# Four modulation vectors moved to VectorE column sums, a third direct tile in each SwiGLU, and ScalarE making half of the modulated inputs

## The chip, the cores and the metric

One core of one Trainium2 chip runs the whole program in one launch. The metric is the device time of one execution in microseconds; before the change it is 2919.62 us, the median of 3 runs (2915.01 to 2922.16). Engines are called TensorE (PE in the rows, its weight loads PEld), VectorE (DVE), ScalarE (ACT), GpSimd (POOL) and the DMA queue of SyncE (SP).

## What is computed

Two post-norm layers over 512 latent and 256 context tokens of 1024 channels. Each layer is a half-step SwiGLU, a token mixer (a bidirectional gated DeltaNet beside a Conformer convolution in layer 0, "even"; grouped-query attention in layer 1, "odd"), and a second SwiGLU; all in float32 precision.

```python
def ffn_sublayer(x, shift, scale, gate, w_gu, w_down, g, b):
    y = swiglu(modulate(x, shift, scale), w_gu, w_down)      # x * (1 + scale) + shift
    return layer_norm(ALPHA * x + 0.5 * gate * y, g, b)
def adaln_modulation(cond, w_ada, b_ada):                    # nine vectors of 1024 per layer
    return jnp.split(silu(cond) @ w_ada + b_ada, 9, axis=-1)
```

There are two conditioning vectors, one for latent and one for context tokens, so that each of the 18 modulation vectors (9 per layer) is a 2x1024 product with a 1024x1024 block of `ada_w` (4 MB).

## The kernel before, in words

The program is first recorded as a list of operations and then ordered by a list scheduler (`Program.order`, L265): it walks all five engines with a price for each operation (`price`, L188), takes the ready one of the lowest rank, and writes one fixed order per engine. Where its plan leaves TensorE idle for too long it puts in a filler, a 128x128 float32 matmul of the identity into a spare piece of PSUM (`keep`; `pair<-ident` in the rows), which computes nothing that is used. All instructions are emitted at L516, so one reads the rows by tile names and shapes: `b` is a PSUM bank, `pair` a spare PSUM tile (fillers also write to it), `p` a page of SBUF, `mods` the modulation vectors, `cA` and `cB` the scale and shift that the modulation uses.

A product in float32 precision is made of three float32r matmuls (`mm3`): high by high, high by low, low by high. So every operand is first split by `halves` (L703) into a high part (ScalarE copies it) and a low part (VectorE subtracts).

**A SwiGLU** (`ffn`, L1095) has 22 inner tiles of 128 channels. The first HEAD = 2 are made directly (`up`): 8 x 2 x 3 matmuls of 256 columns for each of three chunks of 256 tokens (context C_, latents L1 and L2; the last SwiGLU has no context and two chunks). They can start as soon as one chunk of the input is modulated. The other 20 are made by a Strassen-like scheme (`unit`, L1056): 7 block products x 4 x 3 = 84 matmuls of 384 columns (256 in the last SwiGLU). It needs `Blocks` (L612): sums and differences of the whole modulated input, each split into halves, on VectorE and ScalarE; and per unit `left`, which does the same to the weights. Before `Blocks`, the input pages are stored to DRAM (`xd`), and each finished inner tile is stored too (`hd`). Then comes the down projection: three groups of up to six inner tiles, 8 output tiles each, 18 matmuls of 384 columns per output and half, added to the input by VectorE (`residual`). In the tail, the last four inner tiles are multiplied chunk by chunk, and each chunk is normalized (`normalize`) and modulated (`modulate`, L1008) for what follows.

**The modulation vectors** are made in three ways. `ada` (L793) makes the first two. `ada_sum` (L820) scales the eight 128x1024 pieces of `ada_w` on VectorE by the conditioning column and accumulates them (8 operations of 128x1024 per condition), and then sums over the 128 partitions on TensorE: 4 matmuls with 32 columns of ones and 512 moving columns, a ScalarE copy, 4 transposes, 2 to 4 small VectorE adds. It is a generator whose steps are handed out one per unit and one per output tile of the down projection (`extra`), at rank 100 behind their place. `ada_mm` (L854) does the whole product on TensorE: 16 matmuls of 32x512 with the condition as weights, a copy, 4 transposes, an add; it is used inside the two mixers, where VectorE and ScalarE have the smaller matmuls between them.

**`modulate`** writes for each k of 8 channel tiles a plain copy m = z*a+b (GpSimd for three of four k, VectorE for every fourth), the high part of the same (ScalarE), then per pair of k the low part (VectorE, m minus high), and last scales z itself on GpSimd.

Of the kernel before, what the change touches and what calls it, by code (L numbers as in the profile page):

```python
# [13 lines left out]
AF = mybir.ActivationFunctionType  # L14
ALU = mybir.AluOpType
# [98 lines left out]
def cols(v):  # L114
    return math.prod(v.shape[1:])


class Program:
# [69 lines left out]
    def price(self, o):  # L188

        a, f = o.a, o.f  # L190
        o.bytes = 0
        if f == "matmul":
            n = cols(a[2])
            if a[0].shape[0] == 32 and a[1].shape[0] == 128 and "skip_group_check" in o.k:
                return 0.02 + n * 0.00047
            if a[1].dtype == F32R:
                return max(0.112, 0.0045 + n * 0.000442)
            return 0.01 + max(n, cols(a[1])) * 0.00168
        if f == "transpose":
            return max(0.03, a[1].shape[0] * 0.00086)  # L200
        if f == "dma_start":
            o.bytes = math.prod(a[0].shape) * 4
            return 0.45
        n = cols(a[0])
        if f == "tensor_reduce":
            n = cols(a[1])
        psum = any(isinstance(v, View) and v.tile.pool == "psum" for v in a)
        if o.eng == "vector":
            two = sum(isinstance(v, View) for v in a) > 2
            if f in ("tensor_scalar", "memset", "tensor_copy") and not psum and not two:  # L210
                return 0.14 + n * 0.0006
            return 0.15 + n * 0.00104 + 0.05 * (f == "scalar_tensor_tensor")
        if o.eng == "scalar":
            c = 0.168 + n * 0.00084 if psum else 0.205 + n * 0.000825
            return c + 0.17 * isinstance(o.k.get("scale"), View) + 0.37 * ("accum_out" in o.k)
        if f == "memset":
            return 0.03 + n * 0.0009
        return 0.37 + n * 0.0007 if f == "tensor_scalar" else 0.155 + n * 0.0022
# [313 lines left out]
L1 = (CTX, 256, 0)  # L532
# [9 lines left out]
R_ADA, R_WEIGHT, M_POOL = 100, 150, 4  # L542
T_POOL, S_POOL = False, False

HEAD, GROUP, TAIL, EARLY_U = 2, 6, 4, 2


class Feat:
# [116 lines left out]
class Net:  # L665
# [154 lines left out]
    def ada_sum(self, l, i, conds=2):  # L820

        nc = self.nc
        w = self.io["ada_w"][l].rearrange("(k p) n -> k p n", p=128)
        acc = []
        for k in range(8):
            raw = self.page()
            nc.sync.dma_start(raw, w[k, :, 1024 * i:1024 * i + 1024])
            for m in range(conds):
                c = self.cond[:, k, m:m + 1]
                if k == 0:  # L830
                    acc.append(self.page())
                    nc.vector.tensor_scalar(acc[m], raw, c, None, op0=ALU.mult)
                else:
                    nc.vector.scalar_tensor_tensor(acc[m], raw, c, acc[m], op0=ALU.mult, op1=ALU.add)
            yield
        ps = self.bank()
        for e in range(2):
            for m in range(conds):
                q = conds * e + m
                nc.tensor.matmul(ps[32 * q:32 * q + 32, :], self.ones32, acc[m][:, 512 * e:512 * e + 512], start=True, stop=True, skip_group_check=True)  # L840
        P = 64 * conds
        sb = self.page()
        nc.scalar.activation(sb[0:P, 0:512], ps[0:P, :], AF.Copy)
        pt = self.bank()
        for j in range(4):
            nc.tensor.transpose(pt[:, 128 * j:128 * j + P], sb[0:P, 128 * j:128 * j + 128], self.ident[0:P, 0:P])
        for e in range(2):
            for m in range(conds):
                q = conds * e + m
                o = 8 * i + 4 * e  # L850
                nc.vector.tensor_tensor(self.mods[l][:, m, o:o + 4], pt.rearrange("p (j x) -> p x j", x=128)[:, 32 * q, :], self.adab[:, l, o:o + 4], op=ALU.add)
        yield

    def ada_mm(self, l, i):  # L854
# [153 lines left out]
    def modulate(self, c0, n, cond, A, B, ag, ab, tiles=(0, 8)):  # L1008

        nc = self.nc  # L1010
        for p in range(tiles[0] // 2, tiles[1] // 2):
            z = self.xa.pair(p, c0, n)
            h, l = self.xh.pair(p, c0, n), self.xl.pair(p, c0, n)
            m = self.xm.pair(p, c0, n) if self.xm else self.wide(2 * n).rearrange("p (s n) -> p s n", s=2)
            for s in range(2):
                k = 2 * p + s
                a, b = A[:, cond, k:k + 1], B[:, cond, k:k + 1]
                (nc.gpsimd if k % M_POOL else nc.vector).tensor_scalar(m[:, s], z[:, s], a, b, op0=ALU.mult, op1=ALU.add)
                nc.scalar.activation(h[:, s], like(z[:, s], h[:, s]), AF.Identity, scale=a, bias=b)
            nc.vector.tensor_tensor(l, like(m, h), h.bitcast(F32), op=ALU.subtract)  # L1020
            if ag is None:
                nc.gpsimd.tensor_scalar(z, z, ALPHA, 0.0, op0=ALU.mult, op1=ALU.add)
            else:
                for s in range(2):
                    k = 2 * p + s
                    nc.gpsimd.tensor_scalar(z[:, s], z[:, s], ag[:, k:k + 1], ab[:, k:k + 1], op0=ALU.mult, op1=ALU.add)
# [1079 lines left out]
class Kernel(Even, Odd, Final, Net):  # L2106
# [13 lines left out]
    def run(self):  # L2120
        split = [C_, L1, L2]
        self.nc.epoch("p6", 10)
        self.setup()
        A, B = self.small([128, 2, 8], "cA"), self.chunk(0, 0)
        self.new_x()
        for q in range(4):
            k = slice(2 * q, 2 * q + 2)
            self.ada(q, None if q else self.params)
            self.nc.vector.tensor_scalar(A[:, :, k], self.chunk(0, 1)[:, :, k], 1.0, None, op0=ALU.add)
            for c0, n, cond in split:  # L2130
                if not q:
                    self.load_x(range(6)[c0 // 128:(c0 + n) // 128])
                self.modulate(c0, n, cond, A, B, None, None, (k.start, k.stop))
        self.ffn(0, 0, split, 2, self.sub(0, 0, (0, 3)), self.ada_sums(0, 2, 3, 4))
        self.nc.epoch("p4", 16)
        self.even_params()
        self.even(split, self.sub(0, 1, (0, 6)), chain(*(self.ada_mm(0, i) for i in (5, 6, 7, 8))))
        self.nc.epoch("p6", 10)
        self.ffn(0, 1, split, 8, self.sub(0, 2, (1, 0)), self.ada_sums(1, 0, 1, 2))
        self.ffn(1, 0, split, 2, self.sub(1, 0, (1, 3)), self.ada_sums(1, 3, 4, 5))  # L2140
        self.nc.epoch("p4", 16)
        self.odd([L1, L2], self.sub(1, 1, (1, 6)), chain(*(self.ada_mm(1, i) for i in (6, 7, 8))))
        self.ffn(1, 1, None, 8, None, iter(()))
        self.nc.keep = self.nc.tensor.matmul(self.keep, self.ident, self.ident, start=True, stop=True)

# [30 lines left out]
```

## Time and profile before

| | |
|---|---|
| median of 3 runs | 2919.62 us |
| the profiled execution | 2922.82 us |
| its span, first to last instruction | 2921.1 us |
| TensorE busy | 2855.0 us, 98% |
| TensorE weight loads busy | 2654.4 us, 91% |
| VectorE, ScalarE, GpSimd busy | 2050.3, 1124.0, 541.6 us |
| DMA engines, mean busy share | 38%, 119 GB/s |

In the rows below, a group of instructions gives its count behind the x, then the busy time of the group, the mean duration of one, and the idle time before them. A float32 matmul is two records (two passes), a float32r matmul and a transpose are one. Matmuls overlap in the array, so busy time over count is what one costs, not the mean duration. Fillers count as busy TensorE time.

### The profile page before, as it was taken

The page shows a single profiled execution, that of the slowest core. Times are in us where ns is not written, and L with a number is a line of the kernel's source. Part 1 is how long each engine was busy: PE and PEld are TensorE (multiplying, and loading weights), DVE is VectorE, ACT ScalarE, POOL GpSimd, SP SyncE. Part 2 cuts the span into 40 slices and gives each one's busy share as a digit, 9 for nine tenths or more (in the row PEclk, how much of TensorE's full clock was granted, in tenths as well). Part 3 has the DMA queues.
Part 4 walks back from the last instruction along what each step waited for, and adds up shares of the span by engine and source line. Part 5 has one row for each costly group of instructions (what it writes and reads, how often), then busy time and mean ns, then how long its engine had stood idle before and what let it go on. Part 6 is the DMA issues. An engine that isn't in the chain of part 4 may idle for free.

```text
span 2921.1 us, 48213 instructions
## 1 busy us (share of the span) xinstructions
PE 2855.0 (98%) x19173; PEld 2654.4 (91%) x19173; DVE 2050.3 (70%) x3549; ACT 1124.0 (38%) x1952; POOL 541.6 (19%) x652
## 2 busy tenths in 40 slices
PE   9999999999999999999999999999999999999999
PEld 7999999988777899999999999999998777899998
DVE  4877674578877777877675587786547666788854
ACT  4443332143334634443332244343114454455522
POOL 3000000244863605000000230000007331310001
PEclk9999999999999999999999999999999999999999
DMA  7544373134633223344362144345412331144541
GB/s 236 159 135 124 124 214 100 32 116 116 177 94 105 92 80 123 100 129 139 114 220 88 30 146 128 116 136 195 135 49 63 94 129 49 50 139 134 163 130 48
DMA packets 386014, 346.94 MB, mean 119 GB/s; under 512 B 38528, under 2 KB 338813, under 8 KB 385789
## 3 DMA queue, kind: packets, MB, share of 16 engines
q1 hardware_dynamic: 385789, 343.86, 38.0%
q8 instruction: 151, 2.47, 0.4%
q14 instruction: 74, 0.61, 0.1%
HBM read 296.33 MB, written 47.48 MB: 118 GB/s over the span
## 4 chain that ended last, share of the span: by engine, by line
PE 74%; DVE 5%; DMA 2%; POOL 2%; ACT 1%; issue 1%; SPq 0%; DVEq 0%; POOLq 0%; ACTq 0%
PE b L516 70%; PE pair L516 4%; DVE p L516 3%; POOL p L516 2%; ACT p L516 1%; DMA hd<-p 1%; DVE nwt L516 1%; SPq L516 0%; DVE lnS L516 0%; DVE pair L516 0%; DMA xd<-p 0%; DMA p<-hd 0%; DMA p<-in_ffn_w_gu_dram 0%; DMA p<-in_attn_w_out_dram 0%; DMA p<-inv 0%
## 5 line engine op out<-in xcount | busy, mean ns | idle before, releaser
L516 PE MATMUL b<-p,p 128*128 128x384 f32 (+3 forms) x15509 | 2447.5, 317 | 25.9 <-DVE p L516 18.2
L516 PEld LDWEIGHTS b<-p,p 128*128 128x128 f32 x15509 | 2328.1, 189 | 137.1 <-issue 44.6
L516 ACT ACTIVATE p<-p 128x1024 fp32r<-128x1024 f32 (+10 forms) x887 | 708.2, 821 | 1116.1 <-DVE p L516 463.6
L516 DVE TENSOR_TENSOR p<-p,p 128x1024 fp32r<-128x1024 f32 (+6 forms) x942 | 883.1, 959 | 302.2 <-PE b L516 150.5
L516 ACT ACTIVATE p<-b 128x384 f32<-128x384 f32 (+8 forms) x566 | 257.4, 469 | 554.7 <-PE b L516 514.4
L516 POOL TENSOR_TENSOR p<-p 128x512 f32<-128x512 f32 (+1 forms) x26 | 29.9, 1156 | 1535.3 <-ACT p L516 1534.2
L516 DVE SCALAR_TENSOR_TENSOR p<-b,gate,p 128x256 f32<-128x256 f32 (+1 forms) x417 | 168.1, 434 | 201.9 <-PE b L516 201.3
L516 DVE TENSOR_TENSOR p<-p,b 128x384 f32<-128x384 f32 (+3 forms) x392 | 221.8, 581 | 72.8 <-PE b L516 63.5
L516 POOL TENSOR_TENSOR p<-p,p 128x512 f32<-128x512 f32 (+18 forms) x167 | 150.6, 905 | 441.0 <-DMA p<-row 318.4
L516 DVE SCALAR_TENSOR_TENSOR p<-p,cond,p 128x1024 f32<-128x1024 f32 x119 | 150.6, 1279 | 22.4 <-DMA p<-in_ada_w_dram 22.3
L516 PE MATMUL pair<-ident 128*128 128x128 f32 x952 | 131.9, 284 | 9.9 <-DVE pair L516 3.6
L516 PEld LDWEIGHTS pair<-ident 128*128 128x128 f32 x952 | 119.8, 196 | 18.8 <-DVE pair L516 4.9
L516 DVE SCALAR_TENSOR_TENSOR pair<-p,dw,pair 128x783 f32<-128x783 f32 x116 | 120.0, 1035 | 6.9 <-PE pair L516 4.5
L516 POOL TENSOR_SCALAR p<-p,lnag 128x256 f32<-128x256 f32 x112 | 106.8, 962 | 0.3 <-POOL p L516 0.2
L516 DVE TENSOR_TENSOR p<-b,p 128x128 f32<-128x128 f32 (+4 forms) x160 | 68.1, 459 | 52.3 <-ACT p L516 33.2
L516 PEld LDWEIGHTS b<-ident,p 128*128 128x128 f32 (+3 forms) x550 | 63.6, 147 | 37.7 <-issue 16.6
L516 PE MATMUL b<-ident,p 128*128 128x128 f32 (+3 forms) x550 | 87.1, 277 | 10.0 <-DVE p L516 6.4
L516 PE MATMUL pair<-p,p 128*128 128x256 f32 (+3 forms) x515 | 92.2, 315 | 0.0
L516 DVE TENSOR_TENSOR p<-p 128x512 f32<-128x512 f32 (+1 forms) x94 | 63.2, 675 | 34.6 <-PE b L516 32.7
L516 PEld LDWEIGHTS pair<-p,p 128*128 128x128 f32 x515 | 77.2, 190 | 4.6 <-DVE p L516 0.8
L516 PE MATMUL b<-p,ones 128*32 128x128 f32 (+2 forms) x840 | 73.1, 312 | 2.4 <-DVE p L516 1.5
L516 PE MATMUL b<-p,cond 128*32 128x512 f32 (+1 forms) x352 | 69.8, 549 | 5.3 <-DMA p<-in_ada_w_dram 4.9
(168 smaller groups left out, 1135.6 us busy)
## 6 DMA issues: line engine op xcount, KB each, us to landing
p<-in_ffn_w_gu_dram SPq DMA_DIRECT2D x176, 512.0 KB
p<-in_ada_w_dram SPq DMA_DIRECT2D x144, 512.0 KB
p<-in_ffn_w_down_dram SPq DMA_DIRECT2D x96, 384.0 KB
hd<-p SPq DMA_DIRECT2D x54, 384.0 KB
p<-hd SPq DMA_DIRECT2D x27, 768.0 KB
p<-in_even_w_in_dram SPq DMA_DIRECT2D x25, 512.0 KB
xd<-p SPq DMA_DIRECT2D x24, 512.0 KB
p<-xd SPq DMA_DIRECT2D x24, 512.0 KB
```

The lines of the kernel that those rows point to most:

```text
L516: i = f(*[real(x) for x in o.a], **{k: real(x) for k, x in o.k.items()})
```

## The change

- HEAD goes from 2 to 3: in each SwiGLU one inner tile is made directly instead of by a unit.
- `ada_sum` ends in columns: per condition 8 matmuls with a 128x128 block of the sums as weights and one column of ones as the moving operand. They write the vector where the add wants it, so the copy, the transposes and all but one of the adds are gone.
- Four vectors go from `ada_mm` to `ada_sum`: 5 and 6 of layer 0 (from the even mixer to the first SwiGLU), 6 and 7 of layer 1 (from the attention to the SwiGLU ahead of it). 3, 4 and 5 of layer 1 move one SwiGLU: the second SwiGLU makes 0 to 4 of layer 1, the third 5 to 7.
- `modulate` makes m for k = 0, 1, 4, 5 on ScalarE, the others on GpSimd; none on VectorE.
- Two prices of the scheduler change: the 32x512 matmuls, and matmuls of one moving column.

```diff
-                return 0.02 + n * 0.00047
+                return 0.02 + n * (0.00047 if n <= 256 else 0.00085)
...
-            return 0.01 + max(n, cols(a[1])) * 0.00168
+            return 0.01 + (max(n, cols(a[1])) if n > 1 else 64) * 0.00168
...
-HEAD, GROUP, TAIL, EARLY_U = 2, 6, 4, 2
+HEAD, GROUP, TAIL, EARLY_U = 3, 6, 4, 2
...
         ps = self.bank()
-        for e in range(2):
-            for m in range(conds):
-                q = conds * e + m
-                nc.tensor.matmul(ps[32 * q:32 * q + 32, :], self.ones32, acc[m][:, 512 * e:512 * e + 512], ...)
-        ...
+        for m in range(conds):
+            for j in range(8):
+                o = 8 * m + j
+                nc.tensor.matmul(ps[:, o:o + 1], acc[m][:, 128 * j:128 * j + 128], self.ones32[:, 0:1], ...)
+        o = slice(8 * i, 8 * i + 8)
+        nc.vector.tensor_tensor(self.mods[l][:, 0:conds, o], ps[:, 0:8 * conds]..., self.adab[:, l, None, o]..., op=ALU.add)
...
-                (nc.gpsimd if k % M_POOL else nc.vector).tensor_scalar(m[:, s], z[:, s], a, b, op0=ALU.mult, op1=ALU.add)
+                if k % 4 < 2:
+                    nc.scalar.activation(m[:, s], z[:, s], AF.Identity, scale=a, bias=b)
+                else:
+                    nc.gpsimd.tensor_scalar(m[:, s], z[:, s], a, b, op0=ALU.mult, op1=ALU.add)
...
-        self.ffn(0, 0, split, 2, self.sub(0, 0, (0, 3)), self.ada_sums(0, 2, 3, 4))
+        self.ffn(0, 0, split, 2, self.sub(0, 0, (0, 3)), self.ada_sums(0, 2, 3, 4, 5, 6))
-        self.even(split, self.sub(0, 1, (0, 6)), chain(*(self.ada_mm(0, i) for i in (5, 6, 7, 8))))
+        self.even(split, self.sub(0, 1, (0, 6)), chain(*(self.ada_mm(0, i) for i in (7, 8))))
-        self.ffn(0, 1, split, 8, self.sub(0, 2, (1, 0)), self.ada_sums(1, 0, 1, 2))
-        self.ffn(1, 0, split, 2, self.sub(1, 0, (1, 3)), self.ada_sums(1, 3, 4, 5))
+        self.ffn(0, 1, split, 8, self.sub(0, 2, (1, 0)), self.ada_sums(1, 0, 1, 2, 3, 4))
+        self.ffn(1, 0, split, 2, self.sub(1, 0, (1, 3)), self.ada_sums(1, 5, 6, 7))
-        self.odd([L1, L2], self.sub(1, 1, (1, 6)), chain(*(self.ada_mm(1, i) for i in (6, 7, 8))))
+        self.odd([L1, L2], self.sub(1, 1, (1, 6)), chain(*(self.ada_mm(1, i) for i in (8,))))
```

The scheduler then writes a new order for every engine. On TensorE, at the start of the block products of the second SwiGLU, the order before has fillers between the first units (numbers are buffer numbers; a bank `b` is one block product):

```order
L516 MATMUL b_11100<-p_1423_10432,p_1558_11119 128x384
L516 MATMUL b_11100<-p_1423_10432,p_1557_11081 128x384
L516 MATMUL b_11100<-p_1427_10499,p_1557_11081 128x384
L516 MATMUL b_11100<-p_1423_10432,p_1558_11119 128x384
L516 MATMUL pair<-ident_70 128x128 x11
L516 MATMUL b_11111<-p_1529_11163,p_1540_11054 128x384
L516 MATMUL b_11111<-p_1528_11093,p_1541_11091 128x384
L516 MATMUL b_11111<-p_1528_11093,p_1540_11054 128x384
```

and of the change, at the same place, the direct products of 256 columns run up to the first block product:

```order
L516 MATMUL b_11248<-p_1414_10556,p_1502_10741 128x256
L516 MATMUL b_11248<-p_1414_10556,p_1504_10863 128x256
L516 MATMUL b_11248<-p_1418_10590,p_1504_10863 128x256
L516 MATMUL b_11248<-p_1414_10556,p_1505_10882 128x256
L516 MATMUL b_11328<-p_1411_10474,p_1541_11102 128x384
L516 MATMUL b_11328<-p_1415_10506,p_1541_11102 128x384
L516 MATMUL b_11328<-p_1411_10474,p_1542_11142 128x384
```

Behind these rows no filler stands until the down projection. In TensorE's whole order there are 476 fillers before and 430 now; among the block products of the four SwiGLUs 74 before and 6 now, elsewhere 402 and 424.

Also on TensorE, the sums of `ada_sum` stand between block products, one by one. Of before, in the first SwiGLU (`ones` are the weights):

```order
L516 MATMUL b_2158<-p_142_1100,ones_6_76 32x512
L516 MATMUL b_2112<-p_21_646,p_288_2018 128x384
L516 MATMUL b_2158<-p_143_1160,ones_6_76 32x512
L516 MATMUL b_2112<-p_21_646,p_287_1977 128x384
L516 MATMUL b_2158<-p_142_1100,ones_6_76 32x512
```

and of the change (the page `p_154` or `p_155` with the sums is now the weights):

```order
L516 MATMUL b_2262<-p_21_659,p_298_2202 128x384
L516 MATMUL b_2283<-ones_6_76,p_154_1245 128x1
L516 MATMUL b_2262<-p_25_678,p_298_2202 128x384
L516 MATMUL b_2283<-ones_6_76,p_154_1245 128x1
L516 MATMUL b_2262<-p_21_659,p_299_2264 128x384
L516 MATMUL b_2283<-ones_6_76,p_155_1260 128x1 x2
```

Each matmul with one moving column brings a weight block of its own. In all, 34 matmuls of 32x512 with ones and 64 with the condition are gone, 184 of one column are new, and 52 transposes are gone (32 of 128 columns, 20 of 64).

On VectorE, near the end of the first SwiGLU's down projection, residual additions (`gate`) follow each other before:

```order
L516 SCALAR_TENSOR_TENSOR p_468_3184<-b_4575,gate_3192,p_468_3184 128x128
L516 SCALAR_TENSOR_TENSOR p_471_3301<-b_4575,gate_3192,p_471_3301 128x256
L516 SCALAR_TENSOR_TENSOR p_468_3184<-b_4600,gate_3192,p_468_3184 128x128
L516 SCALAR_TENSOR_TENSOR p_471_3301<-b_4600,gate_3192,p_471_3301 128x256
L516 SCALAR_TENSOR_TENSOR p_468_3184<-b_4621,gate_3192,p_468_3184 128x128
L516 SCALAR_TENSOR_TENSOR p_471_3301<-b_4621,gate_3192,p_471_3301 128x256
```

and now scaled sums of `ada_sum` (`cond`) stand between them:

```order
L516 SCALAR_TENSOR_TENSOR p_463_3349<-b_4685,gate_3237,p_463_3349 128x256
L516 TENSOR_TENSOR cB_4712<-cB_4712,mods_9_216 128x16
L516 TENSOR_TENSOR cA_4708<-cA_4708,lngb_186 128x16
L516 SCALAR_TENSOR_TENSOR p_602_4579<-p_615_4688,cond_74,p_602_4579 128x1024
L516 SCALAR_TENSOR_TENSOR p_603_4613<-p_615_4688,cond_74,p_603_4613 128x1024
L516 SCALAR_TENSOR_TENSOR p_460_3221<-b_4710,gate_3237,p_460_3221 128x128
L516 SCALAR_TENSOR_TENSOR p_463_3349<-b_4710,gate_3237,p_463_3349 128x256
```

Between the first and the last residual addition of the first and of the second SwiGLU there are 14 such sums before and 44 now, in the third 7 and 8. Over the whole program there are 42 more of them (161 instead of 119), and the `ada_w` loads of the moved vectors (eight of 512 KB each) move with them; their number and size stay.

## Rows read from the trace of the kernel before

**Rows 1.** The page: busy time by engine, and the granted TensorE clock in 40 slices.

```profile
PE 2855.0 (98%) x19173; PEld 2654.4 (91%) x19173; DVE 2050.3 (70%) x3549; ACT 1124.0 (38%) x1952; POOL 541.6 (19%) x652
PEclk9999999999999999999999999999999999999999
```

**Rows 2.** Busy time by stretch: a down projection, the even mixer, the attention.

```profile
core 0: us, PE busy (x) PEld busy (x) DVE busy (x) ACT busy (x) POOL busy (x), PEclk, DMA share, GB/s
400.00:560.00 160.00, 160.00 (x981) 155.48 (x980) 87.10 (x152) 29.84 (x30) 4.14 (x4) 1.00 0.26 81
660.00:960.00 300.00, 292.49 (x1910) 233.09 (x1910) 238.12 (x290) 117.86 (x232) 179.10 (x238) 0.99 0.42 118
2300.00:2560.00 260.00, 246.71 (x1653) 199.60 (x1652) 171.01 (x480) 126.64 (x300) 74.63 (x63) 0.99 0.26 82
```

**Rows 3.** Groups of TensorE by shape, in units (1260:1440) and in the last SwiGLU (2720:2870).

```profile
L516 PE MATMUL b<-p,p 128*128 128x384 f32 x1002 | 176.4, 337 | 0.3 <-ACT p L516 0.3
L516 PE MATMUL b<-p,p 128*128 128x256 f32 x1275 | 150.4, 281 | 0.0
```

**Rows 4.** TensorE around the start of the units: stretches, and the fillers in them.

```profile
1140.00:1180.00 40.00, 37.01 (x256) 0.96 0.58 178
1700.00:1733.00 33.00, 28.56 (x205) 1.00 0.65 216
...
L516 PE MATMUL pair<-ident 128*128 128x128 f32 x60 | 7.7, 283 | 0.0
L516 PE MATMUL pair<-ident 128*128 128x128 f32 x49 | 6.3, 275 | 0.0
```

**Rows 5.** The chain that ended last, 1150:1175: start, duration, what.

```profile
1154.11 5.33 DMA xd<-p
...
1162.92 6.48 DMA hd<-p
1169.40 0.02 issue
1169.42 1.77 DVE p L516
1171.19 0.04 issue
1171.24 3.12 PE b L516 x11
```

**Rows 6.** Groups by shape, whole run: TensorE's fillers, modulation matmuls and transposes.

```profile
L516 PE MATMUL pair<-ident 128*128 128x128 f32 x952 | 131.9, 284 | 9.9 <-DVE pair L516 3.6 <-ACT p L516 2.8 <-DVE p L516 1.7
L516 PE MATMUL b<-ident,p 128*128 128x128 f32 x498 | 80.3, 281 | 10.0 <-DVE p L516 6.4 <-POOL p L516 1.1 <-DVE inv L516 0.7
L516 PE MATMUL b<-p,cond 128*32 128x512 f32 x224 | 54.8, 605 | 1.0 <-DMA p<-in_ada_w_dram 1.0
L516 PE MATMUL b<-p,ones 128*32 128x512 f32 x68 | 32.4, 605 | 0.0
L516 PE MATMUL b<-ident,p 64*128 64x64 f32 x40 | 5.0, 237 | 0.0
```

**Rows 7.** Timeline of weight loads and matmuls around a matmul of 24 columns (start, us).

```profile
642.96 0.30 PEld L516 LDWEIGHTS b<-gt,cum 128*128 128x128 f32 x2
643.18 0.75 PEld L516 LDWEIGHTS pair<-ident 128*128 128x128 f32 x6
...
643.00 0.37 PE L516 MATMUL b<-gt,cum 128*128 128x24 f32 x2
```

**Rows 8.** Groups by shape in the two mixers (660:960 and 2300:2560): fillers.

```profile
L516 PE MATMUL pair<-ident 128*128 128x128 f32 x78 | 11.4, 285 | 3.7 <-DVE pair L516 3.6
L516 PE MATMUL pair<-ident 128*128 128x128 f32 x191 | 28.7, 287 | 3.8 <-ACT p L516 2.1 <-DVE p L516 1.7
```

**Rows 9.** Groups by shape, whole run: the scaled sums on VectorE.

```profile
L516 DVE SCALAR_TENSOR_TENSOR p<-p,cond,p 128x1024 f32<-128x1024 f32 x119 | 150.6, 1279 | 22.4 <-DMA p<-in_ada_w_dram 22.3
```

**Rows 10.** Groups by shape, whole run: what `modulate` issues.

```profile
L516 DVE TENSOR_TENSOR p<-p,p 128x512 fp32r<-128x512 f32 x156 | 115.7, 749 | 41.9 <-POOL p L516 36.1 <-ACT p L516 5.6
L516 POOL TENSOR_SCALAR p<-p,lnag 128x256 f32<-128x256 f32 x112 | 106.8, 962 | 0.3 <-POOL p L516 0.2
L516 ACT ACTIVATE p<-p,cB,cA 128x256 fp32r<-128x256 f32 x112 | 56.8, 589 | 27.6 <-DVE p L516 27.5
L516 POOL TENSOR_SCALAR p<-p,cA,cB 128x256 f32<-128x256 f32 x84 | 48.4, 583 | 66.3 <-DVE p L516 65.7
```

More of the change, by code (lines that the diff above doesn't have):

```diff
@@ L836, in ada_sum @@
         ps = self.bank()
-        for e in range(2):
-            for m in range(conds):
-                q = conds * e + m
[L840 to L851, printed above, removed]
+        for m in range(conds):
+            for j in range(8):
+                o = 8 * m + j
+                nc.tensor.matmul(ps[:, o:o + 1], acc[m][:, 128 * j:128 * j + 128], self.ones32[:, 0:1], start=True, stop=True, skip_group_check=True)
+        o = slice(8 * i, 8 * i + 8)
+        nc.vector.tensor_tensor(self.mods[l][:, 0:conds, o], ps[:, 0:8 * conds].rearrange("p (m j) -> p m j", j=8),
+                                self.adab[:, l, None, o].to_broadcast([128, conds, 8]), op=ALU.add)
         yield
```

## The prediction

> **What bounds the kernel now.** I read the page's busy times first, then the stretches, the groups by shape, the chain of waits where TensorE stands still, and at last the order of the changed program. TensorE is busy for 2855.0 of 2921.1 us at full clock almost throughout [rows 1]; in a down projection it is busy for all of 160 us, with VectorE at 87.1, and the two mixers leave it 7.5 of 300 and 13.3 of 260 us [rows 2]. But fillers count as busy: 952 records, 131.9 us [rows 6]. So the end is set by the sum of what stands in TensorE's fixed order, fillers and waits included, and I count the change there. Work on another engine costs nothing as long as TensorE's order doesn't wait for it.
>
> All sums are against the profiled execution of 2922.8 us. It is 3.2 us above the median of the runs, and I take 3.2 us off at the end. A measurement of this kernel can tell about 0.3% (9 us) from no change.
>
> **1. A third direct tile.** One tile by a unit is 84 matmuls of 384 columns at 176.4/1002 = 0.176 us, 14.8 us; directly it is 144 of 256 columns at 150.4/1275 = 0.118 us, 17.0 us [rows 3]. That is 2.2 us more in each of three SwiGLUs; in the last one 96 instead of 84 matmuls of 0.118 us, 1.4 us more. **+8.0 us.** Per tile VectorE and ScalarE lose the sums of `left` and gain two halves.
>
> **2. What the third tile covers.** Before the units, TensorE waits for `Blocks`. The chain shows why: the stores of the input and of a finished tile (5.33 and 6.48 us) hold the pages that VectorE needs, and only 1.8 us after the second store does TensorE go on [rows 5]. Around this place TensorE is idle for 3.0 us of 40 and spends 7.7 us on fillers in the second SwiGLU; 4.4 us of 33 and 6.3 us in the third: 21.4 us [rows 4]. The 17 us of new direct work per SwiGLU go in there, as the order shows: no filler is left. A filler costs 2 x 131.9/952 = 0.277 us [rows 6]; the 24 among the first and the last SwiGLU's block products give 6.6 us, the 6 that remain take 1.7 us back. **-26.3 us.** If the cover is less (the tile adds two low parts, three products and one store ahead of `Blocks`), the least is half, -13; nothing speaks for more than -28.
>
> **3. Four `ada_mm` less.** 64 of 112 matmuls of 32x512 at 2 x 54.8/224 = 0.489 us [rows 6]: **-31.3 us**. They stand in the mixers, and it is all won only if those don't wait in their place; the fillers of part 6 are my charge for that, and a half, -16, the other end.
>
> **4. The old sums and transposes.** 34 matmuls with ones at 2 x 32.4/68 = 0.953 us, -32.4 us; 32 transposes at 80.3/498 = 0.161 and 20 small ones at 5.0/40 = 0.125 us, -7.7 us [rows 6]. **-40.1 us.** The sums stand one by one between block products, so this is time on the path. A part of it is overlap that the group's busy time counts twice; I accept that in the range.
>
> **5. The new sums.** 184 matmuls of one column, each with a 128x128 float32 weight block of its own. No row has this shape. The nearest has 24 columns: its two loads start at 642.96 and the next load at 643.18, though its two matmuls have hardly anything to stream [rows 7]. So two loads take 0.222 us, and the load, not the column, is the price. Lower end: 0.125 us, as the small transpose that loads 128 columns in one pass [rows 6]. Upper end: 0.333 us, when the load of the block product behind it is exposed too (half of 0.222 more). I take the nearest row, 184 x 0.222 = **+40.8 us** (23.0 to 61.3). [...]
>
> **6. Fillers elsewhere.** Outside the block products there are 22 more (402 to 424), where the moved modulation work had filled TensorE's waits; the mixers show 78 and 191 records of such in two stretches already [rows 8]. 22 x 0.277 = **+6.1 us** (0 to +20 with the waits that no filler fills).
>
> **7. VectorE's share.** 42 more scaled sums at 1.279 us [rows 9], 54 us. They are hidden: in the first two down projections there are 30 more each, 38 us beside 87 us in a stretch of 160 [rows 2], about 0.78 of it. Behind such a sum in VectorE's queue stands a residual addition, and behind that a PSUM bank; a delay of 1 to 2.6 us is less than the 3.2 us (18 x 0.176) that TensorE takes to fill one further bank of six. If the cover were gone, they would cost what they last. Their DMAs move along: 16 more loads of 512 KB in each of these SwiGLUs are 8.4 MB, some 52 GB/s more over a down projection that moves 81 now and keeps the DMA engines busy for 0.26 [rows 2]. Nothing is late by them.
>
> **8. Modulation.** Per chunk GpSimd now has 8 x 0.962 + 6 x 0.583 = 11.2 us, ScalarE 8 x 0.589 = 4.7; then 10.0 and 12 x 0.589 = 7.1 [rows 10]. GpSimd stays the longest, 1.2 us shorter; the first pair of tiles now waits for four ScalarE operations instead of two, 1.2 us longer. VectorE's idle time for GpSimd here is 36 us in all, so it is near the path; the signs cancel: **0** (-6 to +6).
>
> **Sum:** 8.0 - 26.3 - 31.3 - 40.1 + 40.8 + 6.1 + 0 = -42.8 us. 2922.8 - 42.8 = 2880.0, minus 3.2 for the median: **2877 us**, 1.5% faster.
>
> **The rivals.**
> - *Cheap sums.* One column costs 0.125 us instead of 0.222, because a load hides under the neighbours. 184 x 0.097 = 17.8 us less: 2859 us. For it: the new matmuls stand between block products that stream for 0.176 us. Against: the row of 24 columns.
> - *The waits come back.* The mixers are bound by their chains, so that half of part 3 (15.7 us) turns into idle time, and `Blocks` begins later because its queue has more before it (a third of part 2, 8 us): 2901 us. For it: the two mixers have most of the idle time and of the fillers today [rows 2, 8]. Against: the new order has only 22 fillers more there.
> - *VectorE becomes the bound, and it is slower.* In the first two down projections the 60 additional scaled sums fall onto TensorE's path, 60 x 1.279 = 77 us. Then 2877 + 77 = 2954 us. It decides from the point where VectorE has no idle time left in these stretches, that is where it is 35 us busier than I reckon (160 - 125). For it: its queue is in order, and TensorE's banks are freed by it. Against: 73 us idle there now.
> - *The change doesn't do what it says:* the order shows the 184 matmuls, the missing fillers and the moved sums, so this has no chance of its own.
>
> **How the numbers follow.** Forecast 0.50, cheap sums 0.25, waits back 0.20, slower 0.05. The range takes in the first three: below, 2859 less 6 for the modulation; above, 2901 plus a part of the upper price of part 5: 2853 to 2908. Beyond are the fourth case and the tails, 0.2 at most. Faster by over 0.3% (below 2911) are the first two and most of the third, 0.90; within 0.3% the rest of the third, 0.06; slower 0.04.
>
> **What would show it.** Right: TensorE still at 97 to 98%; no fillers in a stretch of 40 us before the units of the second and third SwiGLU; a group of 368 records with one column and about 41 us; 96 records of 32x512 with the condition and none with ones; VectorE at 120 to 130 of 160 us in the first down projection. Part 5 is wrong if weight loads in front of one-column matmuls follow each other in much less or more than 0.111 us; part 3 if TensorE's idle time in the mixers grows by more than 10 us; part 7 if TensorE shows waits for residual additions in the down projections. A time above 2911 us makes the prediction wrong.

## The result, and the profile after

The changed kernel takes 2873.91 us, the median of 4 runs (2871.84 to 2877.19); before, beside it, takes 2918.24 us (2915.01 to 2922.16). The ratio is 0.9849, with a 95% interval from 0.9831 to 0.9866. The forecast was 2877 us, and its range and the side it gave hold the time. Several of its terms were wrong, though, in both directions, and the experiments below are about these.

The profiled execution of the changed kernel took 2877.19 us, 45.6 us less than that of before. Its page gives the busy times of the engines:

```profile
PE 2821.1 (98%) x19393; PEld 2691.6 (94%) x19393; DVE 2071.8 (72%) x3497; ACT 1139.5 (40%) x1992; POOL 521.5 (18%) x618
```

Against [rows 1], TensorE is busy for 33.9 us less. Its idle time, span less busy time, went from 2921.1 - 2855.0 = 66.1 us to 2875.5 - 2821.1 = 54.4 us: 11.7 us. The two make the 45.6 us. TensorE is still the bound, though VectorE works 21.5 us more.

The groups of the whole run that answer to [rows 6, 9] (fillers, columns of ones, the condition; then VectorE's scaled sums):

```profile
L516 PE MATMUL pair<-ident 128*128 128x128 f32 x860 | 121.0, 286 | 6.1 <-ACT p L516 3.2 <-POOL ident L516 1.6 <-DVE pair L516 0.8
L516 PE MATMUL b<-ones,p 128*128 128x1 f32 x368 | 49.2, 232 | 0.0
L516 PE MATMUL b<-p,cond 128*32 128x512 f32 x96 | 20.1, 605 | 0.0
...
L516 DVE SCALAR_TENSOR_TENSOR p<-p,cond,p 128x1024 f32<-128x1024 f32 x161 | 202.9, 1279 | 18.6 <-DMA p<-in_ada_w_dram 18.5
```

The condition's matmuls fell by 54.8 - 20.1 = 34.7 us, the old sums with ones (32.4 us) are gone, the fillers fell by 10.9 us. The new one-column matmuls show 49.2 us. VectorE's 42 new scaled sums last 1.279 us as before.

The stretches that answer to [rows 2], and those before the units of the second and third SwiGLU that answer to [rows 4]:

```profile
400.00:560.00 160.00, 160.00 (x990) 159.67 (x989) 119.89 (x179) 27.58 (x27) 0.00 (x0) 0.97 0.40 132
660.00:960.00 300.00, 284.82 (x1901) 241.12 (x1901) 251.77 (x297) 122.62 (x241) 190.28 (x244) 0.98 0.34 96
2300.00:2560.00 260.00, 251.80 (x1814) 224.06 (x1813) 189.61 (x484) 137.62 (x309) 72.02 (x63) 0.99 0.24 70
...
1140.00:1180.00 40.00, 40.00 (x296) 1.00 0.57 178
1700.00:1733.00 33.00, 33.00 (x258) 1.00 0.81 255
```

Four things are to be seen. Before the units TensorE no longer stands still; in the second stretch 6 records of fillers (0.8 us) are left. In the down projection VectorE is at 119.89 of 160 us and TensorE doesn't wait. In the two mixers' stretches TensorE's idle time is 15.2 and 8.2 us, where it was 7.5 and 13.3: 2.6 us more together, well under the 10 us that were to speak against part 3. But in the down projection weight loads fill all but 0.3 of the 160 us, and the granted clock is 0.97 there, 1.00 before. The last point was not in the forecast.

Where the clock falls, two stretches of the first down projection and two of the second show it (TensorE alone: busy time, granted clock, DMA share, GB/s):

```profile
440.00:446.00 6.00, 6.00 (x48) 1.00 0.22 91
446.00:450.00 4.00, 4.00 (x16) 0.57 0.47 130
1500.00:1508.00 8.00, 8.00 (x56) 0.97 0.61 214
1508.00:1515.00 7.00, 7.00 (x27) 0.55 0.22 74
```

and the timeline at the first and at the second of these places (start, duration, what), with the rows of the weight loads below:

```profile
440.41 0.42 PE L516 MATMUL b<-p,p 128*128 128x384 f32 x1
440.67 0.28 PE L516 MATMUL b<-ones,p 128*128 128x1 f32 x2
440.81 0.42 PE L516 MATMUL b<-p,p 128*128 128x384 f32 x1
441.06 0.28 PE L516 MATMUL b<-ones,p 128*128 128x1 f32 x2
441.20 0.42 PE L516 MATMUL b<-p,p 128*128 128x384 f32 x1
...
446.07 6.12 PE L516 MATMUL b<-p,p 128*128 128x384 f32 x25
...
1506.46 2.85 PE L516 MATMUL b<-ones,p 128*128 128x1 f32 x18
1509.18 10.99 PE L516 MATMUL b<-p,p 128*128 128x384 f32 x48
...
440.89 0.37 PEld L516 LDWEIGHTS b<-ones,p 128*128 128x128 f32 x2
441.18 0.19 PEld L516 LDWEIGHTS b<-p,p 128*128 128x128 f32 x1
441.29 0.36 PEld L516 LDWEIGHTS b<-ones,p 128*128 128x128 f32 x2
```

A block product with a one-column matmul behind it starts every (441.20 - 440.41)/2 = 0.395 us; the block product alone is 0.176 us [rows 3], so the one-column matmul costs 0.22 us, as much as two weight loads in [rows 7]. That is the price of part 5. But right behind the last of them the granted clock drops, from 1.00 to 0.57 in 446 to 450 us and from 0.97 to 0.55 in 1508 to 1515, although TensorE's records fill all of these stretches: 25 block products take 6.12 us where they would take 25 x 0.176 = 4.40 us, and 48 behind a run of 18 records take 10.99 in place of 8.45. That lies in no term of the sum. Four more such falls follow these matmuls with no idle time ahead of them: the clock is 0.57 in 507 to 510 us, 0.50 in 545 to 548.4, 0.53 in 1579 to 1583 and 0.50 in 1624 to 1628; the six together are 30.7 us long.

### The profile page after: what moved, and what is told of

It reads as the page before. It is cut to its first block, busy times and chain, and to the rows that moved or that the text cites. A ratio compares the mean times of both kernels' runs of the same rounds, so it can differ in the third digit from the quotient of the medians.

```text
span 2875.5 us, 48510 instructions
## 1 busy us (share of the span) xinstructions
PE 2821.1 (98%) x19393; PEld 2691.6 (94%) x19393; DVE 2071.8 (72%) x3497; ACT 1139.5 (40%) x1992; POOL 521.5 (18%) x618
## 4 chain that ended last, share of the span: by engine, by line
PE 56%; DVE 2%; DMA 1%; ACT 1%; POOL 1%; issue 0%; DVEq 0%; SPq 0%; POOLq 0%; ACTq 0%
PE b L516 54%; PE pair L516 2%; DVE p L516 1%; ACT p L516 1%; POOL p L516 1%; DMA p<-hd 0%; DVE nwt L516 0%; DMA p<-in_ffn_w_gu_dram 0%; DVE lnS L516 0%; DMA p<-in_ada_w_dram 0%; DVE st L516 0%; DMA p<-row 0%; DVE kv L516 0%; DVE qv L516 0%; DVE mx L516 0%
## 5 line engine op out<-in xcount | busy, mean ns | idle before, releaser
L516 PE MATMUL b<-p,p 128*128 128x384 f32 (+4 forms) x15773 | 2478.2, 316 | 18.7 <-ACT p L516 7.9
L516 PEld LDWEIGHTS b<-p,p 128*128 128x128 f32 (+1 forms) x15773 | 2354.3, 189 | 89.7 <-issue 16.1
L516 ACT ACTIVATE p<-p 128x1024 fp32r<-128x1024 f32 (+9 forms) x871 | 696.8, 824 | 1092.3 <-DVE p L516 411.1
L516 DVE TENSOR_TENSOR p<-p,p 128x1024 fp32r<-128x1024 f32 (+7 forms) x922 | 858.7, 951 | 266.4 <-PE b L516 138.3
L516 ACT ACTIVATE p<-b 128x384 f32<-128x384 f32 (+7 forms) x557 | 249.5, 465 | 512.8 <-PE b L516 476.5
L516 DVE SCALAR_TENSOR_TENSOR p<-p,cond,p 128x1024 f32<-128x1024 f32 x161 | 202.9, 1279 | 18.6 <-DMA p<-in_ada_w_dram 18.5
L516 PE MATMUL pair<-ident 128*128 128x128 f32 x860 | 121.0, 286 | 6.1 <-ACT p L516 3.2
L516 ACT ACTIVATE p<-p,cB,cA 128x256 f32<-128x256 f32 (+1 forms) x168 | 84.2, 590 | 39.0 <-DVE p L516 39.0
L516 PE MATMUL b<-ident,p 128*128 128x128 f32 (+2 forms) x499 | 78.8, 278 | 10.5 <-POOL p L516 4.6
L516 PEld LDWEIGHTS b<-ident,p 128*128 128x128 f32 (+2 forms) x499 | 58.5, 149 | 27.8 <-issue 8.2
L516 DVE SCALAR_TENSOR_TENSOR p<-p,qw,p 128x772 f32<-128x772 f32 x48 | 61.1, 1278 | 0.4
```

The source lines that it names most:

```text
L516: i = f(*[real(x) for x in o.a], **{k: real(x) for k, x in o.k.items()})
```

## The experiments

Each kernel was compared with before on the same chip; a difference to the changed kernel is taken between medians. The medians of before beside the runs lie between 2918.2 and 2921.9 us, so such a difference can be off by some 4 us. The first six undo or double one part of the change, or extend it.

**Two direct tiles again.**

```diff
-HEAD, GROUP, TAIL, EARLY_U = 3, 6, 4, 2
+HEAD, GROUP, TAIL, EARLY_U = 2, 6, 4, 2
```

> The kernel after the change with two direct tiles again. Theory: the third direct tile takes the place of fillers and idle time ahead of the units in the second and third SwiGLU (26 us) and costs 8 us in matmuls; without it about 18 us more, some 2892 us, with fillers back among the block products. Rival: the fillers went because the modulation and the sums are lighter, and the tile is a mere cost of 8 us; then about 2866 us, and no fillers there.

2893.62 us, ratio 0.9911 [0.9897, 0.9925], 19.7 us more than the change. The fillers come back:

```profile
L516 PE MATMUL pair<-ident 128*128 128x128 f32 x948 | 133.6, 287 | 5.9 <-ACT p L516 3.2 <-POOL ident L516 1.6 <-DVE pair L516 0.7
```

They are 12.6 us more than the change has, in 88 records, and TensorE's idle time is 10.3 us more (2891.8 - 2827.1 = 64.7 us). Parts 1 and 2 give 8.0 - 26.3 = -18.3 us for the third tile: right in size. The places are not those of the forecast, though:

```profile
1130.00:1190.00 60.00, 57.70 (x370) 1.00 0.58 183
1655.00:1755.00 100.00, 92.81 (x689) 0.97 0.40 124
...
L516 PE MATMUL pair<-ident 128*128 128x128 f32 x80 | 12.0, 289 | 0.0
```

Ahead of the second SwiGLU's units idle time and fillers are only 2.3 + 1.5 = 3.8 us, where part 2 had 10.7. Around the start of the third's units they are 7.2 + 12.0 us, 14.0 more than the change has in the same stretch, and in 75 to 105 us, in the first SwiGLU, 3.0 + 3.9 us, where the change has none.

**The four vectors back in the mixers.**

```diff
-        self.ffn(0, 0, split, 2, self.sub(0, 0, (0, 3)), self.ada_sums(0, 2, 3, 4, 5, 6))
+        self.ffn(0, 0, split, 2, self.sub(0, 0, (0, 3)), self.ada_sums(0, 2, 3, 4))
-        self.even(split, self.sub(0, 1, (0, 6)), chain(*(self.ada_mm(0, i) for i in (7, 8))))
+        self.even(split, self.sub(0, 1, (0, 6)), chain(*(self.ada_mm(0, i) for i in (5, 6, 7, 8))))
...
-        self.odd([L1, L2], self.sub(1, 1, (1, 6)), chain(*(self.ada_mm(1, i) for i in (8,))))
+        self.odd([L1, L2], self.sub(1, 1, (1, 6)), chain(*(self.ada_mm(1, i) for i in (6, 7, 8))))
```

The second and third SwiGLU get back 0 to 2 and 3 to 5 of layer 1.

> The kernel after the change with the four moved vectors made by TensorE inside the mixers again. Theory: 64 matmuls of 32x512 and the transposes come back (33 us), 48 matmuls of one column and a few fillers go (11 and 6 us): about 17 us more, some 2891 us. Rival: the mixers have waits that this work filled, so that it costs nothing there; then the 11 us of columns that go show alone, and the time is about 2863 to 2874 us.

2899.6 us, ratio 0.9934 [0.9921, 0.9946], 25.7 us more than the change; the terms of the move make 16.5 us (31.3 + 2.0 for transposes, less 48 x 0.222 = 10.7 of new sums and 6.1 of fillers). The groups of the whole run:

```profile
L516 PE MATMUL pair<-ident 128*128 128x128 f32 x904 | 126.0, 285 | 9.6 <-DVE p L516 3.4 <-ACT p L516 2.6 <-DVE pair L516 1.9
L516 PE MATMUL b<-p,cond 128*32 128x512 f32 x224 | 53.7, 605 | 0.4 <-DMA p<-in_ada_w_dram 0.4
L516 PE MATMUL b<-ones,p 128*128 128x1 f32 x272 | 35.3, 222 | 0.0
```

The condition's matmuls are 33.6 us more and the one-column matmuls 13.9 us less, near their terms. The fillers and the idle time before them are 5.0 and 3.5 us **more** with the four vectors in the mixers; part 6 had charged the move 6.1 us for the opposite. By place, the fillers around the even mixer and around the attention, first of the change (580 to 1120 and 2190 to 2500 us), then of this run (570 to 1130 and 2190 to 2525):

```profile
L516 PE MATMUL pair<-ident 128*128 128x128 f32 x358 | 50.9, 287 | 1.5 <-DVE pair L516 0.8 <-ACT p L516 0.7
L516 PE MATMUL pair<-ident 128*128 128x128 f32 x244 | 34.4, 279 | 2.1 <-ACT p L516 1.7 <-DVE p L516 0.5
...
L516 PE MATMUL pair<-ident 128*128 128x128 f32 x416 | 59.0, 284 | 5.8 <-DVE p L516 3.2 <-DVE pair L516 1.9 <-ACT p L516 0.7
L516 PE MATMUL pair<-ident 128*128 128x128 f32 x224 | 31.2, 280 | 1.4 <-ACT p L516 1.2 <-DVE p L516 0.2
```

In the attention the matmuls of `ada_mm` do take the place of ten fillers (20 records, 3.2 us). In the even mixer they fill nothing: 58 records of fillers come on top of them. The two runs differ in the clock as well, 0.993 here and 0.989 in the change, so the 25.7 us are not the moved work alone.

**The old end of the sums, for all of them.** The thirteen vectors are summed as before: four matmuls with ones (two with one condition), a copy, four transposes, adds.

```diff
-        for m in range(conds):
-            for j in range(8):
-                o = 8 * m + j
-                nc.tensor.matmul(ps[:, o:o + 1], acc[m][:, 128 * j:128 * j + 128], self.ones32[:, 0:1], ...)
+        for e in range(2):
+            for m in range(conds):
+                q = conds * e + m
+                nc.tensor.matmul(ps[32 * q:32 * q + 32, :], self.ones32, acc[m][:, 512 * e:512 * e + 512], ...)
+        ...
```

> The kernel after the change with the old end of ada_sum (matmuls with 32 columns of ones, copy, transposes). Theory: between block products an old matmul took about 1.18 us of TensorE's time and a new one 0.225; thirteen sums are then about 62 us in the old form and 41 in the new one: up to 21 us more, 2880 to 2895 us, less where the four old matmuls happen to stand together. Rival: one-column matmuls cost 0.125 us, so that the new form saves about 39 us; then some 2913 us. Second rival: old and new cost TensorE the same, 2874 us.

2866.06 us, ratio 0.9818 [0.9804, 0.9831]: 7.8 us **faster** than the change. Every theory missed it. The sums' group, and the timeline at two of them:

```profile
L516 PE MATMUL b<-p,ones 128*32 128x512 f32 x92 | 33.5, 604 | 0.3 <-DVE p L516 0.3
...
376.49 1.04 PE L516 MATMUL b<-p,ones 128*32 128x512 f32 x2
377.47 0.44 PE L516 MATMUL b<-p,p 128*128 128x384 f32 x1
377.84 1.04 PE L516 MATMUL b<-p,ones 128*32 128x512 f32 x2
...
508.88 1.07 PE L516 MATMUL b<-p,ones 128*32 128x512 f32 x8
509.88 1.32 PE L516 MATMUL b<-p,p 128*128 128x384 f32 x6
```

At 376 us the sums alternate with block products, one each 377.84 - 376.49 = 1.35 us. At 508 us all four of a vector (8 records) stand together and take 1.07 us, as long as one by itself (1.04 us): with 32 weight columns each (128*32 in the row), these neighbours ran at once. Which happens is an accident of the plan: in the trace of before 30 of the 34 old sums stand alone and four together, here 25 of 46 stand alone and the others in groups of two to four. So 46 old sums show 33.5 us here, not 46 x 0.953 = 43.8, and the clock stays at 1.00 in the down projections' stretches named above. Two hypotheses came from this, tested below: the one-column matmuls lower the clock, and the old sums are cheap if kept together. An alternating pair takes 1.35 us, where the sum (0.98 us to the next start) and the block product alone (0.176) would make 1.16; what the other 0.19 us are is not shown.

**The old modulation.**

```diff
-                if k % 4 < 2:
-                    nc.scalar.activation(m[:, s], z[:, s], AF.Identity, scale=a, bias=b)
-                else:
-                    nc.gpsimd.tensor_scalar(m[:, s], z[:, s], a, b, op0=ALU.mult, op1=ALU.add)
+                (nc.gpsimd if k % M_POOL else nc.vector).tensor_scalar(m[:, s], z[:, s], a, b, op0=ALU.mult, op1=ALU.add)
```

> The kernel after the change with GpSimd and VectorE making the modulated copy again, as before. Theory: GpSimd is the longest in a modulation either way, 1.2 us apart, and the first pair of tiles loses as much: no difference, 2868 to 2880 us. Rival: GpSimd sets the end of every modulation, five times over three chunks, and the change won up to 18 us there; then about 2890 us.

2882.0 us, ratio 0.9871 [0.9856, 0.9887], 8.1 us more than the change; and its runs (2878.44 to 2883.32) all lie above those of the change, though the two intervals overlap. The forecast's 0 was too low; whether the part is worth more than the 6 us at its end isn't shown, for by the ratios the difference is 6.4 us. The fillers grow to

```profile
L516 PE MATMUL pair<-ident 128*128 128x128 f32 x914 | 126.8, 284 | 6.5 <-ACT p L516 3.1 <-POOL ident L516 1.6 <-DVE pair L516 1.4
```

by 5.8 us over the change. That GpSimd's shorter chain counts for more than ScalarE's longer start fits this, but no run parts the two.

**Each one-column matmul twice.** The matmul line stands twice; the second writes the same value over the first.

> The kernel after the change with every one-column matmul issued twice, into the same place. Theory: 0.222 us each for two weight loads, all on TensorE's path: 184 x 0.222 = 41 us more, about 2915 us. Rival, a load hides under the neighbours: 23 us more, 2897 us. Third: they stand in idle time and cost nothing, 2874 us.

2930.42 us (2916.15 to 2947.88, 12 runs), ratio 1.0029 [1.001, 1.0047], 56.5 us more than the change for 184 matmuls, 0.307 us each. The loads alone are 184 x 0.222 = 40.8 us, an estimate from [rows 7]. The rest shows in the granted clock, which is 0.976 to 0.988 over its runs; where two whole sums follow each other, one stretch is

```profile
238.00:258.00 20.00, 20.00 (x80) 0.51 0.10 27
```

TensorE is busy throughout, and yet its granted clock is 0.51 over the 20 us. More one-column matmuls, longer at the low clock: the first hypothesis gains, but this run can't part the clock from the loads.

**All sums on VectorE.** The last three `ada_mm` vectors move as well: 7 and 8 of layer 0 into the first SwiGLU, 8 of layer 1 into the third.

> The kernel after the change with the last three vectors (7 and 8 of layer 0, 8 of layer 1) also summed by VectorE, none by TensorE in the mixers: 40 more scaled sums of 1.28 us on VectorE, of which 32 in the first SwiGLU. Theory: VectorE still has idle time there; 48 matmuls of 32x512 (20 us) go and 40 of one column (9 us) come, with some fillers in the mixers 4 to 11 us less: 2863 to 2870 us. Rival: VectorE has become the bound in the down projections, and the 32 sums add up to 41 us: 2880 to 2915 us.

2914.26 us, ratio 0.9974 [0.9963, 0.9985], 40.4 us more than the change. The first SwiGLU then has seven vectors of nine steps, 63, for its 43 places (19 units and 24 outputs); the other 20 run before its tail. The stretch there (busy time of TensorE, its loads, VectorE, ScalarE, GpSimd; clock), two groups of TensorE in it, and one run of VectorE's scaled sums in the timeline:

```profile
540.00:620.00 80.00, 77.51 (x626) 76.06 (x626) 57.13 (x76) 3.12 (x4) 5.37 (x8) 0.87 0.25 93
...
L516 PE MATMUL pair<-ident 128*128 128x128 f32 x224 | 30.0, 303 | 0.0
L516 PE MATMUL b<-ones,p 128*128 128x1 f32 x96 | 14.6, 286 | 2.5 <-DVE p L516 2.5
...
547.42 16.82 DVE L516 SCALAR_TENSOR_TENSOR p<-p,cond,p 128x1024 f32<-128x1024 f32 x14
```

TensorE fills 30.0 us with fillers until VectorE is done; over the whole run the fillers go from 121.0 to 161.0 us. This is the mechanism of the prediction's third rival, though VectorE is busy for only 57.13 of the 80 us: it decides when the steps no longer fit the places and stand one behind another, not at the load that the change gives.

**The third direct tile alone.** The kernel before, with HEAD = 3 and nothing else.

> The kernel before with the third direct tile alone. Theory: fillers and idle time ahead of the units go, as in the change: 18 us less than the kernel before, ratio about 0.994. Rival: without the lighter modulation the tile only costs its 8 us of matmuls, ratio about 1.003.

2889.76 us, ratio 0.9892 [0.9879, 0.9904], 32 us faster than before; parts 1 and 2 say 18.3. The tile does its part,

```profile
1140.00:1180.00 40.00, 40.00 (x312) 1.00 0.51 162
...
L516 PE MATMUL pair<-ident 128*128 128x128 f32 x818 | 113.7, 284 | 9.9 <-DVE pair L516 3.6 <-ACT p L516 2.8 <-DVE p L516 1.7
L516 PE MATMUL b<-p,ones 128*32 128x512 f32 x68 | 23.1, 605 | 0.0
```

and beside it the plan came out with more of the old sums standing together: their group went from 32.4 us [rows 6] to 23.1, 9.3 us that nobody asked for. The fillers are 18.2 us less than in [rows 6], and TensorE's idle time is 2885.7 - 2830.9 = 54.8 us, 11.3 less. With the 8.0 us that the tiles cost, these make 30.8 of the 35.4 us between the two profiled executions; a clock of 0.996 in place of 0.994 is about the rest.

**One column or 32.** The same matmuls in the same places, but with 32 equal columns of ones as the moving operand; the weights, and so the loads, stay. The add reads one column in 32.

```diff
-                nc.tensor.matmul(ps[:, o:o + 1], acc[m][:, 128 * j:128 * j + 128], self.ones32[:, 0:1], ...)
+                nc.tensor.matmul(ps[:, 32 * o:32 * o + 32], acc[m][:, 128 * j:128 * j + 128], self.ones32, ...)
...
-            return 0.01 + (max(n, cols(a[1])) if n > 1 else 64) * 0.00168
+            return 0.01 + (max(n, cols(a[1])) if n not in (1, 32) else 64) * 0.00168
```

> The kernel after the change with 32 equal columns of ones as the moving operand instead of one, in the same order and place; the weight loads are the same. Theory: the loads set the price of the new sums (0.222 us each) and stay, but the stretches at half clock behind the runs of one-column matmuls come from the array having next to nothing to stream; with 32 columns some or all of them go, 5 to 15 us less, 2859 to 2869 us. Rival: the clock falls because of the many loads, or for another reason, and the same stretches stay: 2874 us. Second rival: the columns cost their streaming: 184 x 2 x 0.027 = 10 us more, 2884 us.

2866.82 us (2861.69 to 2869.75), ratio 0.9807 [0.9789, 0.9826]: 7.1 us faster with 32 times as much to stream. The group, the stretch that answers to 446 us above, the one that answers to 1508 with the 18 records ahead of it, and at last one more place, of the change and of this run:

```profile
L516 PE MATMUL b<-ones,p 128*128 128x32 f32 x368 | 49.5, 251 | 0.0
...
446.00:450.00 4.00, 4.00 (x25) 1.00 0.69 174
...
1504.32 2.09 PE L516 MATMUL b<-ones,p 128*128 128x32 f32 x18
1506.00:1513.00 7.00, 7.00 (x43) 1.00 0.32 83
...
545.00:548.40 3.40, 3.40 (x18) 0.50 0.00 0
541.00:544.40 3.40, 3.40 (x18) 0.50 0.00 0
```

The group costs what it did (49.5 for 49.2 us), so the loads are the price. The second rival's 0.027 us for each record of 32 columns, near a quarter of the 0.111 us at which fillers of 128 columns follow each other in before (22 in 2.45 us, from 639.88 us on), doesn't show: the 368 records are 0.3 us longer together. Of the six places where the clock fell behind these matmuls it stays up in five. At the sixth, 541 us here, it falls as it did, to 0.50. The mean clock of a whole run is 0.989 to 0.991 in the four runs of the change and 0.992 to 0.994 in the five of this kernel. In the profiled executions it goes from 0.989 to 0.992: 0.008 x 2865.7 = 22.9 us of missing clock in place of 0.011 x 2875.5 = 31.6, 8.7 us less, and the two executions differ by 9.7. So with the same weight loads, one moving column in place of 32 is what lowered the clock in those five places. What exactly the clock follows is not shown, and the sixth place says that 32 columns are not always enough.

**Old sums, kept together.** The four matmuls are planned as one operation and come out as neighbours; the copy and the transposes are those of before, the small adds become two.

```diff
+        if f == "rowsums":
+            return 1.1
...
+                if o.f == "rowsums":
+                    ps, ones, *acc = [real(x) for x in o.a]
+                    for q in range(2 * len(acc)):
+                        e, m = divmod(q, len(acc))
+                        nc.tensor.matmul(ps[32 * q:32 * q + 32, :], ones, acc[m][:, 512 * e:512 * e + 512], ...)
+                    continue
...
+        nc.tensor.rowsums(ps[0:64 * conds, :], self.ones32, *acc)
```

> The kernel after the change, with the old row sums planned and issued as one group: the four matmuls with ones stand next to each other in TensorE's order instead of alternating with block products. Theory: next to each other they run at once in the four column parts of the array, 1.1 us per sum (as one group did in the run with the old sums), against 4.7 us when they alternate with block products and 3.6 us for sixteen one-column matmuls; with the transposes ten sums save about 2 us each against the change: some 20 us, 2854 us; against the run with old sums 10 to 25 us. Rival: what the run with the old sums won came from the order elsewhere, not from the sums, and grouping changes nothing: 2866 us.

2841.19 us (2836.95 to 2843.72), ratio 0.9725 [0.9712, 0.9737]: 32.7 us faster than the change, 24.9 faster than the same sums left to the plan. The group, one sum in the timeline, and the down projection's stretch:

```profile
L521 PE MATMUL b<-p,ones 128*32 128x512 f32 x92 | 14.0, 605 | 0.0
...
497.22 1.06 PE L521 MATMUL b<-p,ones 128*32 128x512 f32 x8
...
400.00:560.00 160.00, 160.00 (x1048) 155.78 (x1047) 122.57 (x195) 30.46 (x31) 5.36 (x8) 1.00 0.44 138
```

The sums cost 14.0 us, where one-column sums cost 49.2 and scattered ones 33.5, and the clock is 1.00. TensorE's records in these 160 us rise from 990 to 1048.

**The same, with the last vectors spread.** Vector 8 of layer 0 goes to the second SwiGLU, ahead of 0 to 3 of layer 1; the third SwiGLU makes 4 to 8 of layer 1, and the attention none. No SwiGLU gets more than five vectors, 45 steps.

> Grouped row sums, and two more vectors taken out of the mixers, spread so that no SwiGLU has more steps than places: 8 of layer 0 and 0 to 3 of layer 1 in the second SwiGLU, 4 to 8 of layer 1 in the third. Theory: two TensorE products of 7 to 9 us go, two grouped sums of 1 to 1.6 us come, some fillers return: about 10 us less than with grouped sums alone, 2831 us. Rival: the mixers wait in their place, or VectorE's later queue is late in the third SwiGLU: 2841 us or more.

2835.76 us (2834.18 to 2839.24), ratio 0.9708 [0.9691, 0.9724], 5.4 us under the kernel above and the fastest of all. Two more `ada_mm` are gone; the gain is smaller than expected, and part of it is within the spread of the runs.

## Why the prediction was right, and where its steps were not

The total was right because errors of both signs cancelled, and that they did is luck. In the order of the prediction's parts:

- **Parts 1 and 2, the third direct tile: right in mechanism and sum, not in the places.** -18.3 us by the sum, 19.7 by undoing it. The stretches show the cover itself: no idle time before the units, and no filler but for 0.8 us in the third SwiGLU. But with the rest of the change in place the tile covers 3.8 us in the second SwiGLU, not 10.7, and more than forecast in the third and the first.
- **Part 3 and part 6, the move of four vectors: right in direction, too small.** 16.5 us by the sum, 25.7 measured. The matmuls won what they should. The failing step is part 6's charge: the 22 additional fillers of the order were put down to the moved work, while the kernel with that work put back shows more fillers and more idle time, 8.5 us together, not less. Only the attention behaves as forecast; the even mixer does the opposite. The second rival, that half of part 3 turns into waits, falls too: the idle time of the two stretches grew by 2.6 us, not by 15.7.
- **Part 4, the old sums.** 0.953 us for one is what the trace of before shows on average [rows 6], but it isn't a price of the operation. It is that of a plan in which 30 of 34 alternate with full-width matmuls (1.35 us to the next, of which 0.176 is the block product) and four stand together (1.06 us for the four). The average holds for that plan only: 46 of them in a new plan show 33.5 us, 10.3 less than by the average. The alternative that the change should have been weighed against costs 14.0 us for the same thirteen vectors, and their transposes.
- **Part 5, the new sums.** The price of the loads was right: 0.222 us forecast from [rows 7], 0.22 in the alternating places. The other half of the prediction's sign, a group of about 41 us, was missed: it shows 49.2. That is how a group's busy time counts, and not a price: where the matmuls alternate, two records last 0.28 us and overlap the block products, while the period grows by 0.22; with 32 columns and most of the clock back the group shows 49.5. The missing term is the granted clock, which falls behind the one-column matmuls (0.57 in 446 to 450 us) and slows the block products that follow (25 take 6.12 us in place of 4.40). With 32 columns in place of one, 7.1 us come back. The rival of cheap sums (0.125 us) falls with the 0.22 us.
- **Parts 4 and 5 together: wrong in sign.** The run with the old sums undoes the new form for all thirteen vectors. By the prices of the sum these are 46 x 0.953 = 43.8 and 40 x 0.161 + 12 x 0.125 = 7.9 of transposes against 184 x 0.222 = 40.8: columns are 10.9 us cheaper. Undone, they are 7.8 us dearer. The 10.3 us of the average and the 7.1 us of the clock make up 17.4 of that difference of 18.7.
- **Part 7, VectorE: right.** 119.89 of 160 us (120 to 130 forecast), and no wait of TensorE for it. That the third rival is real shows only when three more vectors are moved.
- **Part 8, modulation: too small.** 0 by the sum, 8.1 by the medians and 6.4 by the ratios. That the signs cancel was a choice without a row. Why the change gains here is not shown.

By undoing one part at a time, the change's parts are worth 19.7 + 25.7 - 7.8 + 8.1 = 45.7 us, and the medians differ by 44.3; by the ratios the four make about 40. But a part's worth depends on the plan around it, as the 32 us of the third tile alone show, and these four numbers are no constants. Why the even mixer needs fewer fillers with fewer `ada_mm` in it was seen but not taken apart.

## What to carry to other kernels

Price a matmul by what it loads as well as by what it streams, and ask what it does to the clock of its neighbours: with a 128x128 float32 weight block of its own, one column cost 0.22 us here, and then some of the clock behind it (0.55 in 1508 to 1515 us, behind 18 records of such matmuls). Matmuls like the old sums, of 32 weight columns each, are worth making neighbours on purpose: four took as long as one (1.06 and 1.04 us), and a planner that scatters them gave back 25 us. And when a total comes out right, undo the parts one by one all the same; here two terms were off by 9 and 8 us on one side and one by 19 on the other.

## What was not expected of the hardware

- TensorE's granted clock fell to about half behind one-column matmuls while TensorE was busy without a gap (0.57 in 446 to 450 us, 0.55 in 1508 to 1515, 0.51 for 20 us with the matmuls doubled), and with 32 columns in the same places in only one of six (0.50 in 541 to 544.4 us). No idle time stands ahead of the six falls of the change, as far as the records show, whose ends are modelled. Another fall of the same trace has some: the clock is 0.50 in 2221 to 2226 us, and TensorE was idle for 4.1 of the 10 us ahead of it.
- Four matmuls of 32 weight columns, 8 records, took 1.06 to 1.07 us as neighbours, and one, 2 records, 1.04 us by itself.
